# Windowed attention on one core: entering the engine loops at once, with GpSimd casting the first q

## Chip, cores, metric

One of the cores of a Trainium2 chip runs the whole kernel. The metric is the device time of one execution in microseconds. Medians are quoted with their number of runs, and differences below about 2 us are not read as differences.

## The reference

```python
B, S, D, W = 4, 4096, 1536, 64            # q, k, v: float32 [B, S, D]
q_w, k_w, v_w = (x.reshape(B, S // W, W, D) for x in (q, k, v))
logits = einsum('bnwd,bnud->bnwu', q_w, k_w) * D ** -0.5
attn = softmax(logits, axis=-1)
out = einsum('bnwu,bnud->bnwd', attn, v_w).reshape(B, S, D)
```

Attention within windows of 64 rows. The kernel works on 32 blocks of 512 rows (4 slots of 128).

## The kernel before

All engines run their own loop over blocks and are tied together by semaphores. A block's q is transposed by TensorE (a product with the identity matrix; pairs of f16 taken as one f32), evacuated, that is copied out of TensorE's result buffers, by VectorE and ScalarE, then k likewise, then the products, the softmax and the product with v. GpSimd issues all loads and stores except the first load and half of the last store; its loads convert f32 to f16 on the way. The tiles `q16`, `k16`, `v16` are single buffers: the next load into one is issued when its present block has been read. The first q alone comes in f32 by SyncE's queue and has to be cast by an engine; q, k and v of the second block are loaded early into spare output buffers and copied ("unstaged") by GpSimd.

```python
def load(name, u, dst, s):                     # casting load, GpSimd's queue
    ...
    nc.gpsimd.dma_start(out=..., in_=...).then_inc(s, 16)

def tensor_unit():                             # one block on TensorE
    ...                                        # await_(g_q), transposes of q; await_(g_k), of k, ...

with tc.tile_critical(no_gpsimd_drain=True):
    raw = rows(qf, 0, SLOTS, SLOTS).rearrange("p h (r d) -> p (h r) d", d=D)
    for sl, s in ((slice(0, 1), d_r0), (slice(1, 2), d_r1), (slice(2, SLOTS), d_r2)):
        nc.sync.dma_start(out=outs[0][:, sl, :], in_=raw[:, sl, :]).then_inc(s, 16)
    nc.vector.memset(ident[:, :], 0.0).then_inc(i_d, 1)
    nc.gpsimd.wait_ge(i_d, 1)
    nc.gpsimd.wait_ge(d_r0, 16)
    nc.gpsimd.affine_select(out=ident[:, :], ...).then_inc(i_p, 1)
    load("k", 0, k16, d_k)
    load("v", 0, v16, d_v)
    load("q", 1, staged(2, 0), d_q1)
    load("k", 1, staged(2, 1), d_k1)
    load("v", 1, staged(1, 0), d_v1)
    load("v", 2, vs, d_vs)
    ...                                        # memsets on VectorE
    nc.tensor.wait_ge(i_p, 1)
    nc.tensor.wait_ge(i_d, 5)
    nc.scalar.wait_ge(i_d, 5)
    nc.scalar.activation(zeros[:, 3:4], ...)   # loads the exp table
    for a, eng in enumerate((nc.vector, nc.scalar)):
        copy = nc.scalar.copy if a else nc.vector.tensor_copy
        for i in range(a, SLOTS, 2):
            eng.wait_ge((d_r0, d_r1, d_r2, d_r2)[i], 16)
            copy(out=q16[:, i, :], in_=outs[0][:, i, :]).then_inc(c_q[a], 1)

    with nc.Fori(0, N, engines=OrderedEngineSet([PE]), head_slot={PE: 0}):
        tensor_unit()
    ...                                        # the same for VectorE and ScalarE
    ...                                        # SyncE: counts tokens out
    for a in range(2):
        sy.wait_ge(c_q[a], 2)
    sy.sem_inc(g_q, 1)                         # TensorE's token for the first q
    ...
    gp.wait_ge(d_q1, 16)                       # GpSimd, after the first issues
    gp.wait_ge(m_q, 1)
    unstage(staged(2, 0), q16, g_q)
    gp.wait_ge(d_k1, 16)
    gp.wait_ge(m_k, 1)
    unstage(staged(2, 1), k16, g_k)
    for u in range(1, N - 1):
        gp.wait_ge(m_q, u + 1)
        load("q", u + 1, q16, d_q)
        ...                                    # store of block u - 1, load of k, of v
```

The softmax here doesn't subtract the row's maximum and nothing guards it: scores larger than these inputs give would overflow.

## Time and profile before

| | before |
|---|---|
| time, median of 3 | 951.46 us (951.34 to 952.49) |
| span of the profiled run | 949.9 us |
| busy share: TensorE / ScalarE / VectorE / GpSimd | 64 / 35 / 30 / 10 % |
| HBM traffic over the span | 302 MB read, 101 MB written, 424 GB/s |
| last half of the first q landed (first consumer starts) | 11.15 us |
| TensorE's first transpose / first evacuation by VectorE | 12.94 / 16.93 us |
| copies of the second block's staged q, k, v | 33.93, 41.20, 48.53 us |

The upper half is the whole execution; the lower half is its first 50 us.

### The profile page before, as it was taken

To read this page: it belongs to the slowest core of one execution; us is meant where nothing else is said; L and a number is where in the kernel's file an instruction comes from. 1 tells how busy PE (TensorE), PEld (TensorE's weight loads), DVE (VectorE), ACT (ScalarE), POOL (GpSimd) and SP (SyncE) were. 2 spreads that over 40 slices of the span, in tenths; PEclk is the share of its full clock that TensorE was granted. 3 is DMA by queue.
4 is the path that set the end of the run, shared out by engine and by line. 5 is a ranking of instruction groups with operands and counts; after the bars stand their busy time and mean duration, and the time that the engine had idled before them with its cause. 6 is when DMAs were issued, how large, how long until landed. Compare 5 with 4: busy or idle time off the path is not lost. (4 is left out here: it accounts for less than half of the span.)

```text
span 949.9 us, 11240 instructions
## 1 busy us (share of the span) xinstructions
PE 612.1 (64%) x4096; PEld 395.3 (42%) x3456; DVE 280.8 (30%) x456; ACT 334.4 (35%) x644; POOL 92.0 (10%) x136
## 2 busy tenths in 40 slices
PE   3776856587565776656865558655577665776582
PEld 2544443354433444423544335443344443444450
DVE  2331413332132331333322333223333133331341
ACT  2442513443233442234432344323343233442252
POOL 2230100100001100101001010010110001100010
PEclk9987978988788987889887888787997788987796
DMA  9999999999999999999999999999999999999996
GB/s 256 216 281 281 228 250 281 281 283 267 236 277 279 284 279 238 263 279 283 283 253 245 280 281 283 272 234 274 279 283 281 243 257 281 280 284 261 233 240 295
DMA packets 26938, 253.34 MB, mean 267 GB/s; under 512 B 2096, under 2 KB 2096, under 8 KB 10544
## 3 DMA queue, kind: packets, MB, share of 16 engines
q0 software_dynamic: 26352, 248.52, 99.8%
q1 hardware_dynamic: 576, 4.72, 1.3%
q14 instruction: 8, 0.07, 0.0%
q8 instruction: 2, 0.03, 0.0%
HBM read 301.99 MB, written 100.66 MB: 424 GB/s over the span
## 5 line engine op out<-in xcount | busy, mean ns | idle before, releaser
L149 PE MATMUL tp<-ident,k 128*128 128x128 f32 x768 | 154.9, 349 | 228.9 <-PEq L215 222.0
L149 PEld LDWEIGHTS tp<-ident,k 128*128 128x128 f32 x768 | 120.2, 182 | 249.9 <-issue 247.3
L161 PE MATMUL lt<-xq,xk 128*128 128x256 f16 x1536 | 216.1, 293 | 0.0
L224 ACT COPY xk<-tp 128x512 f32<-128x512 f32 x96 | 59.3, 618 | 415.1 <-ACTq L215 415.1
L224 DVE COPY xk<-tp 128x512 f32<-128x512 f32 x96 | 66.5, 693 | 379.5 <-DVEq L215 379.5
L161 PEld LDWEIGHTS lt<-xq,xk 128*128 128x128 f16 x1536 | 159.9, 104 | 33.3
L149 PE MATMUL tp<-ident,q 128*128 128x128 f32 x768 | 106.6, 284 | 66.5 <-DVE xq L224 48.9
L149 PEld LDWEIGHTS tp<-ident,q 128*128 128x128 f32 x768 | 88.5, 145 | 100.8 <-issue 100.1
L270 ACT ACTIVATE et<-lt,zeros 32x128 f16<-32x128 f32 x256 | 92.0, 360 | 39.4 <-ACTq L215 36.2
L224 ACT COPY xq<-tp 128x512 f32<-128x512 f32 x96 | 59.4, 619 | 99.6 <-ACTq L215 99.6
L117 PE MATMUL o<-v,et 128*128 128x512 f16 x384 | 93.3, 379 | 0.0
L190 PEld LDWEIGHTS <-et 128*128 128x128 f16 x384 | 30.2, 97 | 151.3 <-issue 114.3
L257 DVE TENSOR_SCALAR out<-o,rs 128x512 f32<-128x512 f32 x128 | 90.2, 747 | 7.7
L224 DVE COPY xq<-tp 128x512 f32<-128x512 f32 x96 | 66.1, 689 | 69.7 <-DVEq L215 69.7
L117 PE MATMUL tp<-v,et 128*128 128x512 f16 x256 | 75.8, 377 | 0.0
L110 POOL DMA_DIRECT2D k<-in_k_dram x31 | 17.4, 561 | 413.4 <-ACTq L222 413.4
L247 DVE RECIPROCAL rs<-sp 128x2 f32<-128x2 f32 x64 | 10.6, 166 | 157.3 <-DVEq L215 157.1
L281 ACT ACTIVATE out<-tp,rs 128x512 f32<-128x512 f32 x64 | 44.0, 688 | 35.8 <-ACTq L215 31.3
L257 DVE TENSOR_SCALAR out<-tp,rs 128x512 f32<-128x512 f32 x64 | 48.1, 751 | 26.2 <-DVEq L215 26.2
L117 PE MATMUL lt<-v,et 128*128 128x512 f16 x128 | 48.3, 377 | 0.0
L281 ACT ACTIVATE out<-o,rs 128x512 f32<-128x512 f32 x64 | 44.0, 688 | 0.0
L281 ACT ACTIVATE out<-lt,rs 128x512 f32<-128x512 f32 x64 | 43.6, 681 | 0.0
(27 smaller groups left out, 109.1 us busy)
## 6 DMA issues: line engine op xcount, KB each, us to landing
out_dram<-out POOLq DMA_DIRECT2D x31, 3072.0 KB, 28.5
k<-in_k_dram POOLq DMA_DIRECT2D x31, 1536.0 KB, 20.6
q<-in_q_dram POOLq DMA_DIRECT2D x30, 1536.0 KB, 21.6
v<-in_v_dram POOLq DMA_DIRECT2D x29, 1536.0 KB, 18.9
vs<-in_v_dram POOLq DMA_DIRECT2D x2, 1536.0 KB, 33.6
out<-in_q_dram SPq DMA_DIRECT2D x2, 768.0 KB, 5.2
out<-in_q_dram SPq DMA_DIRECT2D x1, 1536.0 KB, 9.3
out<-in_q_dram POOLq DMA_DIRECT2D x1, 1536.0 KB, 25.9
```

Source lines behind the costliest of these rows:

```text
L110: nc.gpsimd.dma_start(out=slots(dst, 0, SLOTS, r), in_=rows(src, u * UR, SLOTS, r)).then_inc(s, 16)
L117: return nc.tensor.add_instruction(mybir.InstMatmult(name=nc.get_next_instruction_name(), engine=PE, ins=[low(rhs), low(w)], outs=[low(o)] ...
L149: ins = nc.tensor.transpose(tps[g % 2][:, r, j, :], pairs[:, c * P : (c + 1) * P], ident[:, :])
L161: ins = nc.tensor.matmul(lts[h][:, r, :, :], lhsT=halves(xk, c)[:, r, h, :, w], rhs=halves(xq, c)[:, :, h, :, w], start=(c == 0 and w == 0 ...
L190: ld = nc.tensor.ldweights(w)
L224: copy(out=dst, in_=tps[g % 2][:, :, :, :]).then_inc(f_c[g % 4], 1)
L247: ve.reciprocal(out=rs[:, n : n + R], in_=sp[:, n : n + R]).then_inc(n_d, 1)
L257: ins = ve.tensor_scalar_mul(scaled(u, n, j), bank(n, j), scalar1=rs[:, n : n + 1])
L270: ins = sc.activation(ets[h][s, :, :, s], lts[h][s, :, :, s], EXP, bias=zeros[s, 0:1], scale=scale)
L281: ins = sc.activation(scaled(u, n, j), bank(n, j), COPY, bias=0.0, scale=rs[:, n : n + 1])
```

## The change

Intent: in the kernel before, VectorE and ScalarE cast the first q and only then enter their loops, so the cost of entering lies on the path of the first block. The change lets the three engines enter while q is still on its way; GpSimd, idle then, casts q, and SyncE, which already hands TensorE its tokens (semaphore counts that say "this input is ready"), takes over the waits for the identity, the constants and the casts.

```diff
@@ semaphores
-    c_q = [sem("c_qd"), sem("c_qa")]
-    i_d, i_p, done = sem("i_d"), sem("i_p"), sem("done")
+    i_d, i_p, c_q, done = sem("i_d"), sem("i_p"), sem("c_q"), sem("done")
@@ GpSimd's start
         load("k", 0, k16, d_k)
         load("v", 0, v16, d_v)
-        load("q", 1, staged(2, 0), d_q1)
+
+        for i in range(SLOTS):
+            nc.gpsimd.wait_ge((d_r0, d_r1, d_r2, d_r2)[i], 16)
+            nc.gpsimd.tensor_copy(out=q16[:, i, :], in_=outs[0][:, i, :]).then_inc(c_q, 1)
+            if i == 1:
+                load("q", 1, staged(2, 0), d_q1)
         load("k", 1, staged(2, 1), d_k1)
@@ ahead of the loops
-        nc.tensor.wait_ge(i_p, 1)
-        nc.tensor.wait_ge(i_d, 5)
         nc.scalar.wait_ge(i_d, 5)
         nc.scalar.activation(zeros[:, 3:4], zeros[:, 0:1], EXP, bias=zeros[:, 0:1], scale=1.0)
-        for a, eng in enumerate((nc.vector, nc.scalar)):
-            copy = nc.scalar.copy if a else nc.vector.tensor_copy
-            for i in range(a, SLOTS, 2):
-                eng.wait_ge((d_r0, d_r1, d_r2, d_r2)[i], 16)
-                copy(out=q16[:, i, :], in_=outs[0][:, i, :]).then_inc(c_q[a], 1)
@@ SyncE
-        for a in range(2):
-            sy.wait_ge(c_q[a], 2)
+        sy.wait_ge(i_p, 1)
+        sy.wait_ge(i_d, 5)
+        sy.wait_ge(c_q, SLOTS)
         sy.sem_inc(g_q, 1)
```

## The prediction

> **What bounds the kernel now.** I read the page's slices and queues first, then the opening of the trace in order of time, then the same for GpSimd alone. In the page's slices each digit is a fortieth of the span (23.7 us):
>
> ```profile
> PE   3776856587565776656865558655577665776582
> DVE  2331413332132331333322333223333133331341
> POOL 2230100100001100101001010010110001100010
> DMA  9999999999999999999999999999999999999996
> ...
> q0 software_dynamic: 26352, 248.52, 99.8%
> ```
>
> The transfer engines are busy in all slices but the last; no compute engine is. GpSimd's queue alone takes 99.8% of their span. The page counts SBUF-side bytes; a load reads f32 and writes f16, so each of the 32 blocks moves, on the HBM side, four equal transfers of 4 x 128 x 1536 x 4 bytes = 3.146 MB (q, k, v in, result out). GpSimd's timeline gives their pace: its issue of k for one block stands at 87.33 us and 28 blocks later at 902.53, so a block takes 815.2 / 28 = 29.11 us, or 7.28 us a transfer. That is 12.58 MB / 29.11 us = 432 GB/s.
>
> The opening by engine, VectorE first, then ScalarE, TensorE and GpSimd ("start us, us, engine, line, operation", in brackets the idle time before and its releaser):
>
> ```profile
> 5.53 0.96 DVE L328 CAST q<-out 128x1536 f16<-128x1536 f32 x1 [3.74 <-DMA out<-in_q_dram]
> 11.15 0.96 DVE L328 CAST q<-out 128x1536 f16<-128x1536 f32 x1 [4.66 <-DMA out<-in_q_dram]
> 16.93 0.69 DVE L224 COPY xq<-tp 128x512 f32<-128x512 f32 x1 [4.82 <-DVEq L215]
> ...
> 11.15 1.47 ACT L328 CAST q<-out 128x1536 f16<-128x1536 f32 x1 [2.32 <-DMA out<-in_q_dram]
> 17.33 0.62 ACT L224 COPY xq<-tp 128x512 f32<-128x512 f32 x1 [4.71 <-ACTq L215]
> ...
> 12.94 1.94 PE L149 MATMUL tp<-ident,q 128*128 128x128 f32 x8 [12.94 <-PEq L215]
> 17.76 4.01 PE L149 MATMUL tp<-ident,q 128*128 128x128 f32 x16 [2.88 <-DVE xq L224]
> ```
>
> The last two quarters of q land at 11.15, their casts end at 12.11 and 12.62, and TensorE starts 0.32 us later. Its first transposes are done at 14.88, but the first evacuation starts only at 16.93 and 17.33: 4.82 and 4.71 us after VectorE and ScalarE left their casts, and TensorE idles 2.88 us for it. That is the price of entering the loop, paid after the casts; it is what the change attacks.
>
> Now GpSimd, which issues all further transfers:
>
> ```profile
> 6.59 0.68 POOL L110 DMA_DIRECT2D k<-in_k_dram  x1
> 7.27 0.73 POOL L110 DMA_DIRECT2D v<-in_v_dram  x1
> 7.97 0.58 POOL L110 DMA_DIRECT2D out<-in_q_dram  x1
> ...
> 33.93 2.74 POOL L293 COPY q<-out 128x3072 f32<-128x3072 f32 x1 [23.43 <-DMA out<-in_q_dram]
> 41.20 2.75 POOL L293 COPY k<-out 128x3072 f32<-128x3072 f32 x1 [4.53 <-DMA out<-in_k_dram]
> 43.89 0.55 POOL L110 DMA_DIRECT2D q<-in_q_dram  x1
> 48.53 2.75 POOL L293 COPY v<-out 128x3072 f32<-128x3072 f32 x1 [4.09 <-DMA out<-in_v_dram]
> ```
>
> The second block's q, k, v land at 33.93, 41.20 and 48.53, 7.3 us apart, though issued 0.6 us apart: the queue is served in order and is full. SyncE's first token for the first k, at 19.3 us, and its 7.2 us wait for v, ending at 26.5, put the landings before them at the same pace. So block 2 waits for its data, not for block 1.
>
> **What the Trainium skill says.** "DMA: Bandwidth & Descriptors", Specifications, gives a ceiling of 435 GB/s for the 16 engines; the 432 GB/s above agrees, so there is no slack to fill in the steady part. The same page, Anatomy of one DMA, gives for this path about 2.0 us plus bytes / 436e3; 3.146 MB make 7.2 us apart from the fixed part, and the trace shows 7.3. "Runtime: NRT & Kernel Launch", Instruction fetch mechanics, says that a taken branch to a page not held stalls until it is fetched; the 4.7 to 4.8 us at loop entry fit that, but the trace shows only the gap, not its cause. "GPSIMD Engine Reference", Engine selection, says that one-input elementwise work is roughly at line rate there; the trace's f32 copy of 3072 elements a partition takes 2.74 us, 0.89 ns an element.
>
> **The change, part by part.**
>
> 1. Casts. Two VectorE casts (0.96 us) and two of ScalarE (1.47) go; four on GpSimd come. No GpSimd cast is in the trace; at the copy's 0.89 ns an element, 1536 elements make an estimated 1.37 us each. GpSimd issues v until 8.0, casts slots 0 and 1 until 10.7, issues q of block 2 until 11.3, casts slots 2 and 3 (landed 11.15) until 14.1. The casts end 14.1 - 12.6 = 1.5 us later than now. After the same 0.3 us TensorE starts at 14.4.
>
> 2. Loop entry. VectorE and ScalarE reach their loops at about 2 us, so the 4.8 us end at about 7 and are hidden. TensorE need not wait for the identity (6.64) before entering either. In the warm block at 37.23 us, VectorE's first copy follows TensorE's first transpose by 1.21 us; from the slower first group (1.94 us) I take half plus 0.2, so the first evacuation starts at 14.4 + 1.2 = 15.6 instead of 16.93: 1.3 us earlier. Parts 1 and 2 together: the saved 4.8 us less 2 us that the transposes would have taken anyway less 1.5 for the casts, 1.3 us net.
>
> 3. Where this lead goes. Block 1's q transposes end at about 20.6 instead of 21.9; k has landed (19.3), v lands at 26.5, needed at about 30.5 instead of 31.8. So block 1 ends 1.3 us earlier, near 35.9 instead of 37.2. Block 2's q is unstaged only at 33.93 + 2.74 = 36.67, which leaves TensorE 0.5 us of lead, and its k at 41.20 + 2.75 = 43.95, where TensorE already waits today (idle 2.30 us before 44.24). At 44.24 the lead is zero. Nothing that GpSimd issues next moves: its issues at 43.89 and 51.22 follow landings.
>
> 4. Later issues. q of block 2 goes out 2.8 us later (10.7), the other three about 5.7 us later (14.1 instead of 8.5). Their turn in the queue comes when their forerunner has landed: 26.5 for q, 33.9 for k. The slack is 15 and 19 us, so the transfer engines never see it.
>
> 5. SyncE's three waits instead of two are on events long past but for the casts; the tail is untouched: the last stores are issued at 931.77 and 932.79 after a queue that is full to about 941.
>
> Sum on the path that sets the end: 0 us, within a few tenths.
>
> **Rivals.**
>
> *The lead reaches the end.* 1.3 us less: 950.1. For it: the first block is a true chain. Against: 2.30 us of waiting for staged k erases it.
>
> *GpSimd casts turn out slow, say 3 us each.* Then TensorE starts near 21, block 1 ends near 42, and block 2's k starts about 2 us late. Its follower, k of block 3, is issued at 52.55 today into a queue that still holds the last staged v, q of block 3 (43.89) and a store (51.22), some 15 us of transfers. It would be absorbed; at worst a hole of 1 to 2 us: 953. For it: the GpSimd rate for f32 to f16 is not in the trace.
>
> *Another rhythm.* TensorE's granted clock falls to 0.66 at 45 to 50 us and to 0.5 at times later; a shifted start may move these falls, and the queue does run short now and then (share 0.64 at 83 to 84 us, 0.35 at 902 to 903). Either sign, about 1 us: 950.5 to 952.5.
>
> *Starved queue.* If the late issues left it empty for 5 us, 956; slack of 15 us speaks against.
>
> **Range and chances.** The three times before spread over 1.15 us (951.34 to 952.49). I set the centre 0.2 us below their median for a rhythm that may profit a little: 951.3, and 949.8 to 952.8 for lead, rhythm and spread together. Two per cent is 19 us, more than the whole idle time of transfers: 402.65 MB at 432 GB/s are 932 us of a span of 949.9. Faster 0.01, same 0.98, slower 0.01.
>
> **What would show it.** Right: the first VectorE and ScalarE evacuations near 15.6 and 16 with almost no TensorE idle after its first eight transposes; four GpSimd casts near 1.4 us; block 1 ending about 1.3 us earlier; yet the copies of staged q, k, v still starting at 33.9, 41.2 and 48.5 and a block still taking 29.1 us. Wrong: casts of 2 us and more with TensorE starting after 16; staged landings that shift with their issue; a transfer share below 0.9 between 10 and 40 us; or a block time away from 29.1 us.

## The result

The changed kernel took 951.27 us (median of 4, 950.68 to 952.33), the kernel before 951.64 us beside it (median of 4, 951.34 to 952.49). The ratio is 0.9996, 95% interval 0.9979 to 1.0013: the same. Ratios here are the mean time of one kernel's fast runs over that of the other's of the same rounds (as far as the figures tell, the first, profiled run of a list is left out where more than two are there), so they are not quite the ratio of the medians. For the conversions below, 0.001 of ratio is 0.95 us.

The page of the changed kernel, slices and main queue:

```profile
PE   2776855577565776656865558655577565776682
DVE  1331413332133331333322333223332132331341
POOL 4230100110001100101001010010110001100010
DMA  9999999999999999999999999999999999999997
...
q0 software_dynamic: 26352, 248.52, 99.8%
```

Only the first slice shows the change clearly: GpSimd goes from 2 to 4 tenths, VectorE and TensorE lose one. The transfer row is full as before, and k of the fourth block and of the last are issued at 87.27 and 902.65 us (before: 87.33 and 902.53), so a block takes 29.12 us as against 29.11.

The opening of the changed kernel, the first evacuations of VectorE and ScalarE and the first transposes of TensorE, each from its engine's timeline:

```profile
17.94 0.69 DVE L223 COPY xq<-tp 128x512 f32<-128x512 f32 x1 [16.15 <-DVEq L214]
...
18.77 0.61 ACT L223 COPY xq<-tp 128x512 f32<-128x512 f32 x1 [16.26 <-ACTq L214]
...
16.71 6.00 PE L148 MATMUL tp<-ident,q 128*128 128x128 f32 x24 [16.71 <-PEq L214]
22.93 1.36 PE L148 MATMUL tp<-ident,k 128*128 128x128 f32 x8 [0.23 <-DVE xq L223]
```

The hole in the transposes is gone, as intended: 24 in one run of 6.00 us, where before 8 were followed by 2.88 us of idleness. But they begin at 16.71 instead of 12.94 us. GpSimd's timeline says why:

```profile
8.98 2.89 POOL L313 CAST q<-out 128x1536 f16<-128x1536 f32 x2
11.80 0.56 POOL L109 DMA_DIRECT2D out<-in_q_dram  x1
13.43 2.88 POOL L313 CAST q<-out 128x1536 f16<-128x1536 f32 x2 [1.07 <-DMA out<-in_q_dram]
16.25 0.53 POOL L109 DMA_DIRECT2D out<-in_k_dram  x1
...
34.55 2.74 POOL L292 COPY q<-out 128x3072 f32<-128x3072 f32 x1 [16.34 <-DMA out<-in_q_dram]
41.81 2.75 POOL L292 COPY k<-out 128x3072 f32<-128x3072 f32 x1 [4.52 <-DMA out<-in_k_dram]
44.51 0.55 POOL L109 DMA_DIRECT2D q<-in_q_dram  x1
49.16 2.75 POOL L292 COPY v<-out 128x3072 f32<-128x3072 f32 x1 [4.10 <-DMA out<-in_v_dram]
```

Two casts take 2.89 us together, close to the estimate. The unforeseen part is the bracket at 13.43: GpSimd is held for 1.07 us, by the profile for the last half of q, which had been there at 11.15 in the kernel before. The first block therefore starts its evacuations 1.0 us later than in that profile, not 1.3 us earlier, and TensorE turns to the second block at 38.08 instead of 37.23. All the same the three copies of staged data wait for their loads, as before, and stand 0.6 us later than before; their loads were issued 3.8 to 7.7 us later. (Against the second profile of the kernel before, shown at the end of the experiments, the evacuation is 0.5 us earlier; a difference of this size lies within that kernel's own scatter.) TensorE begins the second block's k at 44.86 (before 44.24), after waiting 2.06 us for it: a difference of 0.62, just that of the landing (41.81 against 41.20).

The rhythm did shift once: q of the fourth block goes out at 68.69 instead of 70.69, where the granted TensorE clock (the share of full speed that the chip allowed) over 60 to 70 us was 1.00 instead of 0.66; that the clock is the cause was not tested. At 87 us, one load later, the two kernels agree again to 0.06 us.

### The profile page after: what moved, and what is told of

It is laid out like the page before. It is cut to its first block, busy times and chain, and to the rows that moved or that the text cites. A ratio compares the mean times of both kernels' runs of the same rounds, so it can differ in the third digit from the quotient of the medians.

```text
span 949.5 us, 11240 instructions
## 1 busy us (share of the span) xinstructions
PE 609.7 (64%) x4096; PEld 393.6 (41%) x3456; DVE 278.7 (29%) x454; ACT 331.3 (35%) x642; POOL 97.4 (10%) x140
## 5 line engine op out<-in xcount | busy, mean ns | idle before, releaser
L148 PE MATMUL tp<-ident,q 128*128 128x128 f32 x768 | 104.0, 280 | 66.6 <-DVE xq L223 47.1
L148 PEld LDWEIGHTS tp<-ident,q 128*128 128x128 f32 x768 | 86.4, 143 | 100.5 <-issue 99.9
L246 DVE RECIPROCAL rs<-sp 128x2 f32<-128x2 f32 x64 | 10.6, 166 | 157.8 <-DVEq L214 157.6
L109 POOL DMA_DIRECT2D v<-in_v_dram x29 | 20.5, 706 | 238.2 <-DVEq L255 238.2
```

Of the source, the lines that this page charges most:

```text
L109: nc.gpsimd.dma_start(out=slots(dst, 0, SLOTS, r), in_=rows(src, u * UR, SLOTS, r)).then_inc(s, 16)
L148: ins = nc.tensor.transpose(tps[g % 2][:, r, j, :], pairs[:, c * P : (c + 1) * P], ident[:, :])
L246: ve.reciprocal(out=rs[:, n : n + R], in_=sp[:, n : n + R]).then_inc(n_d, 1)
```

## The experiments

The theory (T1 in the expectations): the transfers set the end; lead or lag of the first block dies where the second block waits for its staged data. The main rival (T2): gain from entry and loss from the slow casts both reach the end and cancel. A second pair (T3 against T4) is about the late landing of q: the fetch of loop code, or chance. Every edit is against the changed kernel; the last run is the kernel before itself.

### Control

> The changed kernel again, unaltered, as the control. If the transfers set the end (T1), 951.3 us within 1. If the late landing of the first q (last half seen at 13.43 us where the kernel before had 11.15) comes from the loop code being fetched at the same time (T3), it is again after 13 us; if it was chance (T4), near 11.2 us.

No edit. 952.08 us (median of 4) against 950.76 of before (median of 7), ratio 1.0012 (0.9996 to 1.0029). The last half of q is cast from 13.31 us, as in the first profile (13.43); VectorE's first evacuation at 17.82. So the late landing repeats; how much of it is chance in the kernel before, the last experiment shows. This ratio is also the measure for those that follow: 1.0012 is "nothing".

### Half of the change: casts on GpSimd, loops entered after them

```diff
+        nc.tensor.wait_ge(c_q, SLOTS)
+        nc.vector.wait_ge(c_q, SLOTS)
+        nc.scalar.wait_ge(c_q, SLOTS)
         with nc.Fori(0, N, engines=OrderedEngineSet([PE]), head_slot={PE: 0}):
```

> GpSimd casts as in the change, but TensorE, VectorE and ScalarE wait for all four casts ahead of their loops, so the entry is paid after them. T1 (transfers set the end): the first VectorE evacuation comes at about 19 us (casts end near 14.2, plus 4.8), staged q, k, v are still copied at 34, 41.3 and 48.6, total 951.3 within 1. T2 (entry gain and cast loss reach the end and cancel): 3 to 5 us slower, 954 to 956. T3: the last half of q lands near 11.2 us, because no loop code is fetched beside it; T4: anything between 11 and 13.5.

951.72 us (median of 4), ratio 1.0013 (0.9993 to 1.0033). VectorE's and GpSimd's timelines of this run:

```profile
21.32 0.69 DVE L223 COPY xq<-tp 128x512 f32<-128x512 f32 x1 [19.53 <-DVEq L214]
...
12.11 2.88 POOL L313 CAST q<-out 128x1536 f16<-128x1536 f32 x2 [0.89 <-DMA out<-in_q_dram]
```

The last half of q is there 1.2 to 1.3 us sooner than with early entry, and still the first evacuation is 3.4 us later (21.32 against 17.94): the entry, paid after the casts. It was expected at about 19; VectorE evacuated 6.3 us after the end of the casts (14.99), not 4.8. Counted from the landing of the last half, the first evacuation takes 9.2 us here and 4.5 in the changed kernel, so entering early is worth 4.7 us to the first block (TensorE, held too in this run, is a small part of it: it started 0.7 us after the casts). And the total is that of the control. T2 asked for 954 to 956; it falls, narrowly here (the slowest of the four runs took 953.51), clearly in the next two experiments.

### More than the change: no casts at all

```diff
-        for sl, s in ((slice(0, 1), d_r0), (slice(1, 2), d_r1), (slice(2, SLOTS), d_r2)):
-            nc.sync.dma_start(out=outs[0][:, sl, :], in_=raw[:, sl, :]).then_inc(s, 16)
+        load("q", 0, q16, d_r0)
...                                   # the four casts go; the identity waits for no data
-        sy.wait_ge(c_q, SLOTS)
+        sy.wait_ge(d_r0, 16)
```

> The first q comes by a casting load on GpSimd's queue straight into its fp16 tile: no casts, loops entered at once. TensorE starts near 10.5 us instead of 16.7, a lead of 6 us. T1: the lead is gone at the second block's k, transfers start no earlier, so total 950.5 to 951.5. T2: 945 to 946.

950.84 us (median of 4), ratio 1.0002 (0.9985 to 1.0019). TensorE started at 12.65 us, not at 10.5 as expected, but that is still 4.06 us ahead of the changed kernel. VectorE's and GpSimd's timelines:

```profile
13.89 0.69 DVE L223 COPY xq<-tp 128x512 f32<-128x512 f32 x1 [12.09 <-DVEq L214]
...
34.20 2.74 POOL L292 COPY q<-out 128x3072 f32<-128x3072 f32 x1 [27.93 <-DMA out<-in_q_dram]
41.46 2.75 POOL L292 COPY k<-out 128x3072 f32<-128x3072 f32 x1 [4.52 <-DMA out<-in_k_dram]
```

The staged q and k, and v at 48.76 us, were copied within 0.4 us of the changed kernel's. T2's 945 to 946 is excluded. The kernel with the earliest first block of all gains nothing that these runs resolve, so an earlier first block alone makes no faster kernel here.

### Doses of delay in the first block

```diff
         load("v", 2, vs, d_vs)
+        for i in range(8):                                  # also 3 and 24
+            nc.gpsimd.wait_ge(c_q, SLOTS + i)
+            nc.gpsimd.tensor_copy(out=pad[:, :], in_=outs[0][:, i % SLOTS, :]).then_inc(c_q, 1)
...
-        sy.wait_ge(c_q, SLOTS)
+        sy.wait_ge(c_q, SLOTS + 8)
```

`pad` is a tile that nothing reads. All load issues come ahead of it, so only TensorE's start moves.

> Eight more GpSimd casts into an unused tile before SyncE may give TensorE its token, after all load issues: TensorE starts about 12 to 13.6 us later, near 30 us. T1: the queue holds work until about 56 us, q of the third block is issued near 55.5 us instead of 44.5, so nearly all is absorbed: 951 to 955. T2: the delay reaches the end, 963 to 965.

> As with eight, but 24 more casts: TensorE starts near 53 us, about 36 us later than in the changed kernel. T1: the queue is dry from about 56 us until q of the third block can be issued, some 20 to 25 us later: 972 to 978. T2: the whole delay, about 987.

> Three more casts ahead of TensorE's token. The runs with 8 and 24 (TensorE about 14.1 and 38.3 us later, cost some 5 and 30 us) put the slack of the first block's chain at 8 to 9 us. With three, TensorE starts 4.5 to 6.5 us later, inside the slack: 951.5 within 1. If a part of any delay always reached the end (5 of 14, a third), 953 to 954.

| extra casts | first VectorE evacuation | later than control | time | ratio (95%) | cost by ratio |
|---|---|---|---|---|---|
| 0 (control, 4 runs) | 17.82 us | - | 952.08 | 1.0012 (0.9996 to 1.0029) | 1.1 |
| 3 (4 runs) | 24.17 | 6.4 | 952.33 | 1.0012 (0.9995 to 1.0028) | 1.1 |
| 8 (4 runs) | 31.94 | 14.1 | 956.34 | 1.0055 (1.0038 to 1.0072) | 5.2 |
| 24 (2 runs) | 56.14 | 38.3 | 981.22 | 1.0310 (1.0289 to 1.0331) | 29.5 |

14.1 - 5.2 and 38.3 - 29.5 give 8.9 and 8.8 us: the first block may be that late at no cost, and beyond it each microsecond costs one (24.3 us of cost for 24.2 of delay between the two). If the control's 1.1 us is taken off as "nothing", the slack is 10 us; the runs don't fix it closer than that. A delay of 6.4 us, several times what the change moves, costs nothing that these runs resolve. The transfers show the same. With 24 extra casts (stretches of time and their length; then busy time and count of TensorE's matmuls and weight loads, of VectorE, ScalarE and GpSimd; then the granted clock, the share of the transfer engines, which can come out a little over 1, and GB/s, which count the f16 bytes that a load delivers, half of what it reads):

```profile
40.00:54.00 14.00, 0.00 (x0) 0.00 (x0) 0.00 (x0) 0.00 (x0) 13.43 (x10) 1.00 1.04 215
54.00:56.00 2.00, 1.10 (x6) 1.13 (x7) 0.00 (x0) 0.00 (x0) 0.51 (x1) 1.00 0.43 86
56.00:82.00 26.00, 21.78 (x154) 14.54 (x134) 10.70 (x17) 12.20 (x23) 6.23 (x4) 1.00 0.00 0
```

TensorE had done nothing until 54.90 us, and the transfers ran at full share up to 54. They stop when the six loads that GpSimd issued ahead have come in, and stand still for 26 us, until GpSimd may issue q of the third block at 81.27. Lost transfer time is what the kernel pays for, not lost compute time. My sizes were too small here: 951 to 955 and 972 to 978 were expected, 956.3 and 981.2 measured, because I had put the slack at 11 us or more (queue dry at about 56 us, q of the third block due at 44.5).

### Doses of delay in the issues

```diff
                 load("q", 1, staged(2, 0), d_q1)
+        nc.gpsimd.memset(pad[0][:, :], 0.0).then_inc(c_q, 1)
+        for i in range(5):                                  # also 12
+            nc.gpsimd.wait_ge(c_q, SLOTS + 1 + i)
+            nc.gpsimd.tensor_copy(out=pad[1][:, :], in_=pad[0][:, :]).then_inc(c_q, 1)
         load("k", 1, staged(2, 1), d_k1)
```

> GpSimd fills and copies an unused tile (five copies of 2.75 us and one memset) after the casts of q and before it issues k of the second block, which so goes out near 32 us instead of 16.25; TensorE's start is unchanged. T1: that load's turn comes at about 34.5 us, so nothing is lost: 951.3 within 1. Rival (a late issue costs what it is late): up to 966.

> The same with twelve copies: k of the second block is issued near 51 us, past its turn at 34.5. T1: the queue is dry for 16 to 18 us and the time grows by that much, to 966 to 970. If there is slack elsewhere in the transfers, less than that.

With five copies k of the second block went out at 33.18 us (16.25 in the changed kernel): 954.44 us (median of 4), ratio 1.0033 (1.0016 to 1.0051). With twelve it went out at 52.41: 973.99 us (median of 2), ratio 1.0234 (1.0214 to 1.0255). Both are above what I expected. The costs by ratio are 3.1 and 22.3 us; 33.18 - 3.1 and 52.41 - 22.3 both give 30.1 us (31.2 with the control's 1.1 us taken off). That is an estimate of the moment by which the load must be issued. The stretches of the run with twelve copies:

```profile
20.00:32.00 12.00, 10.47 (x83) 8.20 (x81) 3.33 (x5) 4.60 (x9) 11.75 (x5) 1.00 1.04 218
32.00:34.00 2.00, 1.93 (x13) 0.42 (x6) 0.41 (x2) 1.79 (x6) 1.94 (x2) 1.00 0.56 117
34.00:52.00 18.00, 3.62 (x21) 0.52 (x7) 4.16 (x7) 3.38 (x6) 17.63 (x7) 0.70 0.00 0
52.00:60.00 8.00, 2.44 (x11) 2.10 (x12) 0.69 (x1) 0.51 (x1) 5.13 (x5) 0.50 0.83 160
```

The engines run out of work at about 33 us, although the load before is seen as landed, in the control, at 34.75 (in this run 34.6, by the profile's list of issues): the last bytes move before the signal. And after the issue at 52.41 nothing moves before 53, and the share is only 0.83 over the 8 us from 52: a newly issued load needs time before its first bytes. I had taken the signal for the turn. The slack of this issue in the changed kernel is 30.1 - 16.25 = 13.9 us (15 with the control taken off), not 19; the change stays inside it.

### Fewer bytes

```diff
-            out=rows(of, u * UR, SLOTS, R), in_=slots(outs[u % NO], 0, SLOTS, R)
+            out=rows(of, u * UR, R, R), in_=slots(outs[u % NO], 0, R, R)
```

> Wrong result on purpose: the 31 full stores write only the first two of four slots, half their bytes; all work of the engines is unchanged. T1: each block saves half of a 7.28 us transfer, 31 x 3.64 = 113 us, so about 838 if the chain of one block through the engines is short enough, or somewhat more. If not the transfers but the chain of work sets the pace: near 951.

Wrong on purpose (half of each full store is left out). 840.3 us (median of 2, 837.11 and 843.49), ratio 0.8829. The page of before, then that of this run:

```profile
HBM read 301.99 MB, written 100.66 MB: 424 GB/s over the span
```

```profile
DMA  9999999999999999999999999999999999999995
...
HBM read 301.99 MB, written 51.90 MB: 420 GB/s over the span
```

With 48.8 MB less to move, and every compute instruction kept, 111 us go; the transfers are as full as before and the rate is the same to 1%. This is the direct proof of what bounds the kernel (two runs, 6.4 us apart, but the effect is seventeen times that). It also shows that the engines' chains would allow about 12% less.

### Which early entry delays the first q

```diff
+        nc.vector.wait_ge(d_r2, 16)       # first kernel: TensorE alone enters early
+        nc.scalar.wait_ge(d_r2, 16)
```

```diff
+        nc.tensor.wait_ge(d_r2, 16)       # second kernel: VectorE and ScalarE alone
```

> The changed kernel with VectorE and ScalarE held ahead of their loops until q has landed; TensorE enters at once. If the fetch of loop code delays q (T3) and ScalarE's and VectorE's part of it matters, the last half of q lands earlier than in the changed kernel (13.3 us in its profiles), at about 12.1 as with all three held; if TensorE's fetch alone does it, it stays at 13.3.

> The reverse: TensorE held until q has landed, VectorE and ScalarE enter at once. T3 with TensorE's fetch as the cause: the last half of q lands near 12.1 us; with VectorE's and ScalarE's as the cause: 13.3 us.

> The kernel before, unaltered, once more. If its early landing of q (11.15 us) belongs to the kernel it is again within 0.3 us of that; if the scatter from run to run is that large (T4), it may be anywhere up to 13.5.

These were single looks (952.08, 952.40 and 949.98 us, state unknown), read for landings only. Two things can be read: when GpSimd starts the identity, for which it waits for the first quarter of q, and the tenth of a microsecond in which SyncE's queue has its last packet of the first q.

| kernel | enter early | identity starts | last packet of q |
|---|---|---|---|
| before, two profiles | none before the first quarter; TensorE after it, once the identity is there | 5.81, 6.00 | 10.6, 11.7 |
| casts only | none | 5.92 | 11.6 |
| VectorE and ScalarE early | those two | 6.16 | 12.8 |
| TensorE early | TensorE | 7.17 | 12.8 |
| changed kernel, control | all three | 7.07, 7.22 | 13.0, 12.9 |

With TensorE entering early the first quarter comes about 1 us later (0.8 to 1.4 in the table), whatever the others do; all five dose runs, which have it too, lie at 6.96 to 7.61. With either kind of early entry the last packet comes later, at 12.6 to 13.3 in all ten profiles that have one (the table's, the five dose runs and the run with half stores), against 10.6 to 11.7 in the three that have none; together they do little more than one. So the question that I had put, which of the two it is, has the answer: each. The cast of the last half began at 13.26 us with TensorE early and at 13.20 with the other two. It starts 0.4 to 0.5 us after that packet in all ten. One caution: in seven of the ten it also starts 0.80 to 0.81 us after GpSimd's preceding issue, so steadily that GpSimd's own sequence may set a floor there; the runs do not separate the two for the cast. The packets themselves are late whatever GpSimd does then.

The queues of the changed kernel between 2 and 6 us show what moved there (queue 1 is SyncE's; packets, MB, share of the 16 engines):

```profile
q1 hardware_dynamic: 217, 1.24, 90.9%
q8 instruction: 1, 0.02, 1.5%
q14 instruction: 2, 0.02, 1.0%
```

In the kernel before, the same stretch has queue 1 alone (228 packets, 1.30 MB, 95.2%); its instruction packets come at 10 us and later. The packet on queue 8 stands near 4 us in the kernel with TensorE early, and at 17 where TensorE is held; the packets on queue 14 go with VectorE and ScalarE. That instructions are fetched beside q is shown; that they are the loops' code is read from the times at which they move with the entries. That the fetch is the cause of the delay is likely but not shown: no run fetches without entering. One point speaks for caution: in the kernel before the packet on queue 8 comes at 10.6 and 10.3 us, still beside q, and its last packet of q is no later than in the kernel with casts only, where none comes that early. The kernel before also shows the scatter: the cast of its last half began at 12.17 us, outside the 0.3 us that I had set around 11.15, so about 1 of the 2.3 us by which the changed kernel's landing is later than the first profile may be chance. Its first evacuation came at 18.48 us, later than the changed kernel's 17.94.

## Why the prediction was right

The mechanism was right: the first block's time does not reach the end. That the measured 951.27 lies 0.03 us from the centre of 951.3 is luck, as the same kernel took 952.08 in the control; and of its own signs, block 1 ended 0.9 us later instead of 1.3 earlier, and TensorE started after 16 us, half of what it had named as a sign of being wrong (the other half, slow casts, did not come).

**What bounds it.** Right, and proved by bytes: half of the stores gone is 111 us gone (the prediction's 7.28 us a transfer, halved and taken 31 times, is 113). One support was weaker than it looked. The 432 GB/s are counted on the HBM side, while the skill's 435 is the ceiling of the ports of SBUF, the on-chip memory; over these ports the page shows a mean of 267 GB/s, since loads arrive as f16. So the agreement of the two numbers alone does not show that no slack is left; the full rows, the doses and the half stores do.

**Casts, part 1.** The estimate was 1.37 us each; they take 1.45. Right but for 0.08.

**Loop entry, part 2.** The hole in TensorE's transposes went, as said. The sum of parts 1 and 2 failed: a lead of 1.3 us was forecast, against the profile of before it was a lag of 1.0 us. The failing step is the landing of the last half of q, taken as "landed 11.15" and left there; with early entry it comes at 13.43. With that moment and the measured casts in the forecast's own sum, TensorE starts at 13.43 + 2.88 + 0.3 = 16.6; it does at 16.71. One profile of before was also too few for a term of 1 us: its second one has the landing 1.0 and the first evacuation 1.5 us later. The 4.8 us of entry are no fixed price either: in that second profile VectorE came 5.4 us after its cast and ScalarE 3.6 after its own.

**Where the lead goes, part 3.** Right, though it had a lag to swallow instead of a lead. First evacuations between 13.89 us (no casts) and 24.17 (three more casts) leave k of the fourth block, issued more than 60 us later, at 87.19 and 87.26. The staged copies were forecast at 33.9, 41.2 and 48.5 and stand 0.6 us later; what takes these 0.6 us up by 87 us was not looked into.

**Later issues, part 4.** Right that nothing is lost; the slack was mis-sized. It is 13.9 to 15 us for k, not 19: the turn comes near 30 to 31 us instead of 33.9, and the issue itself went out at 16.25 instead of 14.1. The load's turn begins when the engines run dry, near 33 us less the lead a load needs, not when its forerunner is signalled.

**SyncE's waits and the tail, part 5.** The last half-stores are issued at 931.77 and 931.89 us in the two kernels; nothing to correct.

**Rivals.** "The lead reaches the end" falls with the kernel without casts. "Another rhythm" was seen, 2 us at 70 us, and gone at 87. The slow-cast rival did not come, but the run with three more casts is its case: TensorE at 22.93 us, absorbed. The doses put the limit at about 9 to 10 us.

## What to carry to other kernels

Where one resource is full from the third microsecond to the last few, a change at the start is worth only what it does to that resource: ask whether it begins earlier, moves less or stands idle less, and if none of these, forecast zero however real the local gain is. A slack is best measured by two doses beyond it: cost against delay then has slope one, and the crossing is the slack. And code that is fetched travels on the same engines as data, so an entry moved to an idle moment may delay the load that everyone is idle for.

## What the Trainium skill lacked or had wrong

- "Runtime: NRT & Kernel Launch", Instruction fetch mechanics, tells of the stall of an engine that branches to code it does not hold, and this fits it (3.4 us later first evacuation when the loops are entered after the casts). It does not say what a fetch may do to data under way, and no page gives a size for it: with TensorE entering early the first quarter of q was usable at 6.96 to 7.61 us instead of 5.81 to 6.16 (that the fetch is the cause is not shown).
- "GPSIMD Engine Reference", Engine selection, calls one-input work roughly line-rate but this section has no time for a cast. Here f32 to f16 of 128 x 1536 took 1.45 us, 0.94 ns an element, against 0.96 us on VectorE and 1.47 on ScalarE.
- No page says which side's bytes count when a load casts on the way. With f32 loads that arrive as f16, the 16 engines were full at 432 GB/s counted on the HBM side and at a mean of 267 counted on the SBUF side.
- "DMA: Bandwidth & Descriptors", Anatomy of one DMA, gives a fixed part of about 2.0 us, mostly completion. The runs agree roughly: the queue ran dry near 33 us behind a load that the control saw landed at 34.75. By the costs, its successor had to be issued by 30.1 to 31.2. The page does not draw the consequence that a successor must be issued some microseconds ahead of its forerunner's signal, here 3.6 to 4.6 (34.75 less these, an estimate from different runs).
